# A kernel's own account of VectorE's time: shorter prices, a catch-up after forced steps, and one more chunk for the seven-product pair

## The chip, the cores and the metric

The kernel runs on one core of one Trainium2 chip. The metric is the device time of one execution in microseconds (us), the median of several runs. TensorE (PE in the profile) multiplies matrices, VectorE (DVE) and ScalarE (ACT) work element by element, GpSimd (POOL) does little here, and SyncE (SP) issues nearly all DMAs.

## What is computed

The reference is one step of a two-layer streaming encoder over 1024 prompt rows and 32 sample rows, with 1024 channels. Cut to what matters, each layer does this:

```
mod = silu(c) @ w_ada[i] + b_ada[i]            # 6 vectors a layer: shifts, scales, gates
h   = rmsnorm(x) * (1 + sc1) + sh1
mix = layer 0: spatial gating, (u * (W_s v + b)) @ w_out
      layer 1: trailing means over 2, 4, 8, 16 rows minus the row, then a map for each group
x   = x + gt1 * rmsnorm(mix)
h   = rmsnorm(x) * (1 + sc2) + sh2
x   = x + gt2 * rmsnorm(square(relu(h @ w_up)) @ w_down)     # 1024 -> 4096 -> 1024
```

Everything is float32. The last 15 inputs of the pooling mixer and the normalised v of the sample rows are outputs too.

## The kernel before

**Tiles.** Channels lie on the partitions. The 1056 rows are three tiles of 384, 384 and 288 columns (t = 0, 1, 2; the last has the sample rows). Each float32 operand is split into a high part, rounded by ScalarE, and a low part, subtracted on VectorE, and a product takes three matmuls (high by high, high by low, low by high: `products`, lines 1047 to 1049).

**Order of the large products.** First v of the gating mixer (`v_mm`, `v_end`), then u, the gate and the output map (`sgu_item`, `gate`: matmuls at line 1401, their input `vl` loaded at line 1355), then both feed-forward nets. A feed-forward net is cut into eight chunks of 512 hidden channels, c = 0 to 7. The list `passes` (lines 374 to 383) says in which order chunks meet tiles: an entry is (layer, first chunk, tiles, number of chunks). Some entries take tiles 0 and 1 together (`PAIR`). There `pair_item` (from line 1551) writes h @ w_up as a 2 by 2 block product with seven block products in place of eight (lines 1586 to 1588), on sums of blocks: `combos` builds the sums of h, `quads` (line 494) those of the weights. The products by w_down are plain. In layer 0 the pair takes chunks 3 to 7, in layer 1 chunks 2 to 7. What remains of chunks 0 to 2 is done for single tiles, and tile 2 takes all its chunks alone, after the pair.

**Weights.** `stream` holds all loads in order: weights, and the pieces of w_ada ("wide" pieces and their folds, `do_ada`, with a small matmul at line 649), which `some_ada` strews between the chunks. Raw pieces have three buffers; the split parts sixteen slots.

**The planner.** The order in which instructions are written decides who waits, since each engine works in order (a scheduling layer may still move some of them). The kernel plans with an account, `time`, of two sums: `time["pe"]` grows by `tick` at each product, `time["dve"]` by a price for each VectorE instruction, set in `on_dve` (lines 74 to 87) as a fixed part plus elements over a rate:

```
    tt = on_dve(nc.vector.tensor_tensor, 0.16, 930.0)
    stt = on_dve(nc.vector.scalar_tensor_tensor, 0.16, 840.0)
```

Work that must only be done by some later time (normalising, residual additions, pooling, output) stands in generators, `fillers`. After each product `weave` takes one or two steps of the weight stream, unless VectorE is ahead in the account (`stream_waits`), and then filler steps for as long as the account of VectorE stands behind TensorE's:

```
        while time["dve"] < time["pe"] and fillers:
            if not pull():
                break
```

A step may set a gate: the next one then opens only when `time["pe"]` has passed. Before a tile's first chunk of a layer, `run_ffn` calls `finish`, which pulls all that is left of that tile's filler at once:

```
    def finish(tag):
        while any(f[0] == tag for f in fillers):
            pull(True)
```

The fillers that matter here: `ffn0_t` (from the mixer to the input of layer 0's net for tile t), `ffn1_t` (`to_pool`: from layer 0's net through the pooling mixer to the input of layer 1's net), `combos`, and `state`, `sgu_state` (line 1276), which for four quarters loads `vst` and `gvb`, multiplies them on VectorE and stores the product. Its tiles, and `vl`, come from the three buffers of the tag x3.

Of the kernel before, what the change touches and what calls it, by code (L numbers as in the profile page):

```python
# [35 lines left out]
def tile_stream_encoder_step(  # L36
# [25 lines left out]
    nc = tc.nc  # L62
# [5 lines left out]
    time = {"pe": 0.0, "dve": 0.0}  # L68
# [5 lines left out]
    def on_dve(op, fixed, rate):  # L74
        def run(out, *args, **kw):
            n = 1
            for k in out.shape[1:]:
                n *= k
            time["dve"] += fixed + n / rate
            return op(out, *args, **kw)  # L80

        return run

    tt = on_dve(nc.vector.tensor_tensor, 0.16, 930.0)
    stt = on_dve(nc.vector.scalar_tensor_tensor, 0.16, 840.0)
    ts = on_dve(nc.vector.tensor_scalar, 0.1, 930.0)
    turn32 = on_dve(nc.vector.transpose, 0.1, 930.0)

    def pool(name, **kw):
        return ctx.enter_context(tc.tile_pool(name=name, bufs=1, reuse_waits="tile", **kw))  # L90
# [52 lines left out]
    def ps_ms(name):  # L143
        return psum.tile([P, 512], F32, tag="pm", bufs=3, name=name)
# [207 lines left out]
    def w_chunk(n):  # L352
        l, c, tiles, m = passes[n]
        for j in range(4 * m):
            f = 4 * c + j
            add_w(
                ("up", n, j),
                ffn_w_up[l][:, f * P : (f + 1) * P].rearrange("(k p) f -> p k f", p=P),
                (8, P),
                ("one", "two")[j % 2] if tiles == PAIR else "w",  # L360
            )
        w = 256 // m
        for q in range(4 * m):
            add_w(
                ("dn", n, q),
                ffn_w_down[l][c * 512 : (c + m) * 512, q * w : (q + 1) * w].rearrange(
                    "(j p) d -> p j d", p=P
                ),
                (4 * m, w),
            )  # L370

    every = list(range(NT))
    PAIR = every[:2]
    passes = [(0, 0, [0], 2), (0, 2, [0], 1)]
    passes += [(0, c, [1], 1) for c in range(3)]
    passes += [(0, c, PAIR, 1) for c in range(3, 8)]
    passes += [(0, c, [NT - 1], 2) for c in (0, 2, 4, 6)]
    passes += [(1, 0, [0], 2)]
    passes += [(1, c, [1], 1) for c in range(2)]
# [6 lines left out]
    def some_ada(n):  # L386
        for _ in range(min(n, len(rest))):
            add, l, j = rest.pop(0)
            add(l, j)
# [29 lines left out]
    for n, (l, c, tiles, m) in enumerate(passes):  # L419
        w_chunk(n)  # L420
        if tiles == PAIR:
            some_ada((5, 2)[l])
        elif l == 0 and tiles != [NT - 1] and c > 0:
            some_ada(c + 1 if tiles == [1] else 2)
    some_ada(99)
# [120 lines left out]
    def ada_finish(l, sl, view):  # L546

        nk = 2 * view.shape[1]
        m = mod[:, l, 2 * sl : 2 * sl + nk, :].rearrange("p (s h) v -> p s h v", h=2)
        b = bT[:, l * 48 + 2 * sl : l * 48 + 2 * sl + nk].rearrange("p (s h) -> p s h", h=2)  # L550
        tt(out=m, in0=view, in1=b.unsqueeze(3).broadcast_to([P, nk // 2, 2, NV]), op=ALU.add)
        which, k0 = sl // 4, 2 * (sl % 4)
        slot = {1: (0, 0), 2: (1, 1), 4: (2, 2), 5: (3, 3)}.get(which)
        if slot is not None:
            cf, gi = slot
            for v in range(NV):
                stt(
                    out=coef[:, l, cf, v, k0 : k0 + nk],
                    in0=mod[:, l, 2 * sl : 2 * sl + nk, v],
                    scalar=1.0 if cf in (0, 2) else 0.0,  # L560
                    in1=g_of(l, gi)[:, k0 : k0 + nk],
                    op0=ALU.add,
                    op1=ALU.mult,
                )
# [40 lines left out]
    def do_ada(l, sl, q, r, w):  # L605
        nq = w // 128
        if q == 0:
            aas = [
                work.tile([P, 512], F32, tag="aa", bufs=2, name=f"aa{l}_{sl}_{w}_{i}")
                for i in range(nq // 2)  # L610
            ]
            ada_acc[0] = [aas[v * nq // 4][:, v * w % 512 :][:, :w] for v in range(NV)]
        aa = ada_acc[0]
        for c in range(8 // nq):
            for v in range(NV):
                x = r[:, c * w : (c + 1) * w]
                k = csil[:, 8 // nq * q + c, v : v + 1]
                if q == 0 and c == 0:
                    with tc.issue_after(last_lo[("v", 1, 3)].ins):
                        ts(aa[v], x, k, None, op0=ALU.mult)  # L620
                else:
                    stt(out=aa[v], in0=x, scalar=k, in1=aa[v], op0=ALU.mult, op1=ALU.add)
        if q < nq - 1:
            return


        ns = nq // 2
        i = sl * ns % 4
        if i == 0 and state["folds"]:
            run_deferred(True)  # L630
        for v in range(NV):
            turned = r[:, v * w : (v + 1) * w]
            turn32(turned, aa[v])
            time["dve"] += 0.16 + w / 840.0
            nc.vector.tensor_reduce(
                out=part[:, i : i + ns, v],
                in_=turned.rearrange("p (s b m) -> p s b m", s=ns, m=32),
                op=ALU.add,
                axis=AX.X,
            )  # L640
        if i + ns < 4:
            return
        state["folds"] = 1

        def fold():
            state["folds"] = 0
            pa = ps_ms(f"ada{l}_{sl}")
            for c in range(4):
                mm(
                    pa[32 * c : 32 * c + 32, :16],  # L650
                    quad,
                    part.rearrange("p s v (h c) -> p c (s v h)", c=4)[:, c],
                    start=True,
                    stop=True,
                    tile_position=(0, 32 * c),
                    skip_group_check=True,
                )
            y = pa[:, :16].rearrange("p (s v h) -> p s h v", s=4, v=NV)
            ada_finish(l, (sl + 1) * ns - 4, y)

        defer(fold, fold_lag[0])
# [3 lines left out]
    def defer(step, us=None):  # L665

        at = 0.0 if us is None else max(time["pe"], time["dve"]) + us
        deferred.append((at, step))

    def run_deferred(force=False):  # L670
        n = len(deferred)
        while n > 0 and (force or deferred[0][0] <= time["pe"]):
            deferred.pop(0)[1]()
            n -= 1
# [39 lines left out]
    def stream_step():  # L714
# [17 lines left out]
        if kind == "w":  # L732
            do_w(key, r)
        elif kind == "wide":
            do_ada(*key, r, 512)
        elif kind == "ada":
            if k < first_ada:
                do_ada_pe(*key, r)
            else:
                do_ada(*key, r, 256)  # L740
        else:
            do_x(key, r)
# [35 lines left out]
    def pull(force=False):  # L778

        def open_(f):
            return force or gates.get(f[0], 0.0) <= time["pe"]

        if sticky:
            f = sticky[-1]
            if not open_(f):
                return False
            sticky.pop()
        else:  # L790
            f = next((f for f in list(fillers)[:2] if open_(f)), None)
            if f is None:
                return False
        try:
            step = next(f[1])
        except StopIteration:
            fillers.remove(f)
            return True
        if step is True:
            sticky.append(f)  # L800
        elif step is not False:
            gates[f[0]] = max(time["pe"], time["dve"]) + step
        return True
# [12 lines left out]
    def finish(tag):  # L816
        while any(f[0] == tag for f in fillers):
            pull(True)


    def spread(t, ss, tag, out, dg):
# [729 lines left out]
    def pair_item(p, after, ends):  # L1551
# [48 lines left out]
        def up(jp):  # L1600
# [10 lines left out]
            if jp == 0:  # L1611
                flush()
                finish("combos")
# [56 lines left out]
        if passes[p + 1][2] != PAIR:  # L1670
            finish(f"ffn{l}_{NT - 1}")
            fillers.append(late_norm.pop())
# [277 lines left out]
    def run_ffn(l, after):  # L1950
        for p, (pl, c, tiles, m) in enumerate(passes):
            if pl != l:
                continue
            ends = [t for t in tiles if not any(q[0] == l and t in q[2] for q in passes[p + 1 :])]
            if tiles == PAIR:
                pair_item(p, after, ends)
                continue
            for t in tiles:
                if c == 0:
                    if any(f[0] == f"ffn{l}_{t}" for f in fillers):  # L1960
                        flush()
                    finish(f"ffn{l}_{t}")
                ffn_item(p, t, after if t in ends else None)
# [158 lines left out]
```

## Time and profile before

| what | value |
|---|---|
| median of 3 runs | 2157.3 us (2157.04 to 2158.1) |
| the profiled execution, its own time | 2154.9 us |
| its span, first to last instruction | 2153.1 us |
| TensorE busy | 2102.8 us |
| weight loads of TensorE (PEld) | 2032.5 us |
| VectorE busy | 1560.3 us |
| ScalarE busy | 1041.6 us |
| mean granted TensorE clock | 0.99 |
| read from and written to memory | 274.76 MB and 30.66 MB |

The span is the time between the first and the last instruction of the profiled execution; 1.8 us of its own time lie around it, and that time is 2.4 us under the median. Busy time of TensorE overlaps between matmuls that follow each other, so that a matmul's mean duration is longer than the distance between two starts. The clock column gives the share of the full TensorE clock that was granted.

### The profile page before, as it was taken

To read this page: it belongs to the slowest core of one execution; us is meant where nothing else is said; L and a number is where in the kernel's file an instruction comes from. 1 tells how busy PE (TensorE), PEld (TensorE's weight loads), DVE (VectorE), ACT (ScalarE), POOL (GpSimd) and SP (SyncE) were. 2 spreads that over 40 slices of the span, in tenths; PEclk is the share of its full clock that TensorE was granted. 3 is DMA by queue.
4 is the path that set the end of the run, shared out by engine and by line. 5 is a ranking of instruction groups with operands and counts; after the bars stand their busy time and mean duration, and the time that the engine had idled before them with its cause. 6 is when DMAs were issued, how large, how long until landed. Compare 5 with 4: busy or idle time off the path is not lost.

```text
span 2153.1 us, 32925 instructions
## 1 busy us (share of the span) xinstructions
PE 2102.8 (98%) x12858; PEld 2032.5 (94%) x12858; DVE 1560.3 (72%) x2756; ACT 1041.6 (48%) x1833; POOL 22.4 (1%) x44
## 2 busy tenths in 40 slices
PE   8999999999999999999998999896999999999998
PEld 6878999999999999999998999896999999999998
DVE  6778837567778857878777887849677768579554
ACT  5634431233456545334455756555445454365555
POOL 0000000000000000000000000000000000001100
PEclk9999999999999999999999999998999999999999
DMA  8576524353445443334335775643342323238873
GB/s 290 169 256 210 179 81 136 97 163 109 122 129 167 138 147 121 105 98 128 108 122 146 214 221 145 191 131 104 89 142 90 91 86 101 69 113 224 203 188 92
DMA packets 424050, 307.59 MB, mean 143 GB/s; under 512 B 47023, under 2 KB 387287, under 8 KB 423893
## 3 DMA queue, kind: packets, MB, share of 16 engines
q1 hardware_dynamic: 422964, 304.19, 47.2%
q8 instruction: 101, 1.65, 0.3%
q0 software_dynamic: 896, 1.28, 0.2%
q14 instruction: 57, 0.46, 0.1%
q10 hardware_dynamic: 32, 0.01, 0.0%
HBM read 274.76 MB, written 30.66 MB: 142 GB/s over the span
## 4 chain that ended last, share of the span: by engine, by line
PE 90%; DVE 5%; DMA 2%; ACT 2%; issue 1%; DVEq 0%; ACTq 0%
PE pg L1048 10%; PE pg L1047 10%; PE pg L1049 10%; PE pf L1047 5%; PE pf L1048 5%; PE pf L1049 5%; PE pu L1047 3%; PE pu L1049 3%; PE pu L1048 3%; PE po L1047 3%; PE po L1049 3%; PE po L1048 3%; PE pfa L1586 3%; PE pfa L1588 3%; PE pfa L1587 3%; PE pv L1073 2%
## 5 line engine op out<-in xcount | busy, mean ns | idle before, releaser
L1047 PE MATMUL pg<-fh,wh_dn 128*128 128x384 f32 (+1 forms) x968 | 314.7, 326 | 0.9 <-DVE acc L80 0.9
L1048 PE MATMUL pg<-fl,wh_dn 128*128 128x384 f32 (+1 forms) x968 | 312.9, 323 | 0.0
L1049 PE MATMUL pg<-fh,wl_dn 128*128 128x384 f32 (+1 forms) x968 | 311.9, 323 | 0.0
L80 DVE TENSOR_TENSOR wl_dn<-raw,wh_dn 128x1024 fp32r<-128x1024 f32 x148 | 181.1, 1224 | 140.3 <-ACT wh_dn L533 92.9
L1047 PE MATMUL pf<-hh,wh_up 128*128 128x288 f32 (+1 forms) x832 | 262.4, 316 | 10.0 <-ACT hh L1007 8.4
L1048 PE MATMUL pf<-hl,wh_up 128*128 128x288 f32 (+1 forms) x832 | 260.8, 314 | 0.0
L1049 PE MATMUL pf<-hh,wl_up 128*128 128x288 f32 (+1 forms) x832 | 260.1, 313 | 0.0
L533 ACT ACTIVATE wh_dn<-raw 128x1024 fp32r<-128x1024 f32 x148 | 156.7, 1059 | 152.2 <-PE pf L1048 65.1
L80 DVE SCALAR_TENSOR_TENSOR aa<-raw,csil,aa 128x512 f32<-128x512 f32 (+1 forms) x364 | 206.2, 620 | 4.5 <-DMA raw<-in_w_ada_dram 4.4
L80 DVE TENSOR_TENSOR acc<-acc,pg 128x384 f32<-128x384 f32 (+1 forms) x256 | 134.7, 531 | 85.7 <-PE pg L1049 84.4
L1047 PEld LDWEIGHTS pg<-fh,wh_dn 128*128 128x128 f32 x968 | 181.5, 188 | 2.6 <-DVE acc L80 1.3
L1048 PEld LDWEIGHTS pg<-fl,wh_dn 128*128 128x128 f32 x968 | 181.7, 188 | 1.0 <-DVE fl L80 0.2
L1049 PEld LDWEIGHTS pg<-fh,wl_dn 128*128 128x128 f32 x968 | 181.6, 188 | 0.0
L533 ACT ACTIVATE wh_up<-raw 128x1024 fp32r<-128x1024 f32 x104 | 110.2, 1059 | 127.1 <-PE pg L1048 76.2
L80 DVE TENSOR_TENSOR wl_up<-raw,wh_up 128x1024 fp32r<-128x1024 f32 x104 | 126.8, 1220 | 61.1 <-ACT wh_up L533 60.6
L1047 PEld LDWEIGHTS pf<-hh,wh_up 128*128 128x128 f32 x832 | 158.5, 191 | 12.6 <-ACT hh L1007 9.2
L1048 PEld LDWEIGHTS pf<-hl,wh_up 128*128 128x128 f32 x832 | 158.4, 190 | 1.1 <-DVE hl L80 0.9
L1049 PEld LDWEIGHTS pf<-hh,wl_up 128*128 128x128 f32 x832 | 158.8, 191 | 0.1
L1047 PE MATMUL pg<-fx,wh_dn 128*128 128x288 f32 (+1 forms) x392 | 121.8, 311 | 0.0
L1048 PE MATMUL pg<-fx,wh_dn 128*128 128x288 f32 (+1 forms) x392 | 121.7, 311 | 0.0
L1049 PE MATMUL pg<-fx,wl_dn 128*128 128x288 f32 (+1 forms) x392 | 121.4, 310 | 0.0
L1047 PE MATMUL po<-ush,wh_o 128*128 128x384 f32 (+1 forms) x288 | 92.6, 322 | 0.0
(408 smaller groups left out, 5112.3 us busy)
## 6 DMA issues: line engine op xcount, KB each, us to landing
raw<-in_ffn_w_up_dram SPq DMA_DIRECT2D x148, 512.0 KB, 4.0
raw<-in_ffn_w_down_dram SPq DMA_DIRECT2D x148, 512.0 KB, 4.1
raw<-in_w_ada_dram SPq DMA_DIRECT2D x90, 512.0 KB, 4.2
raw<-in_sgu_w_in_dram SPq DMA_DIRECT2D x40, 512.0 KB, 4.0
xd<-acc SPq DMA_DIRECT2D x8, 1536.0 KB, 7.4
raw<-in_sgu_w_out_dram SPq DMA_DIRECT2D x24, 512.0 KB, 3.6
xo_r<-xd SPq DMA_DIRECT2D x32, 384.0 KB, 4.1
vd<-vt SPq DMA_DIRECT2D x32, 256.0 KB, 4.4
```

Source lines behind the costliest of these rows:

```text
L80: return op(out, *args, **kw)
L533: act(out=wh, in_=r, func=AF.Copy)
L1047: mm(ps[:, :n], wh, rh, start=i == 0, stop=False)
L1048: mm(ps[:, :n], wh, rl, start=False, stop=False)
L1049: mm(ps[:, :n], wl, rh, start=False, stop=i == last)
L1073: mm(ps[:m, :], a_h, wh[:, o : o + 512], start=k == 0, stop=False)
L1586: mm(ps[:, :n], wh[:, o], rh, start=first and k == 0, stop=False, skip_group_check=True)
L1587: mm(ps[:, :n], wh[:, o], rl, start=False, stop=False, skip_group_check=True)
L1588: mm(ps[:, :n], wl[:, o], rh, start=False, stop=k == HK - 1, skip_group_check=True)
```

## The change

Three things change.

The prices of VectorE's instructions in the account become smaller. For 512 elements a `stt` goes from 0.77 to 0.67 us, for 1024 elements a `tt` from 1.26 to 1.15 us.

`finish` brings the account of TensorE up to 3 us behind VectorE's when it has pulled its steps.

In layer 0 the pair takes chunk 2 as well: the single entries of chunk 2 for tiles 0 and 1 go. `some_ada` puts six wide pieces behind each pair chunk of layer 0 but the last in place of five, and one behind the last.

```diff
-    tt = on_dve(nc.vector.tensor_tensor, 0.16, 930.0)
-    stt = on_dve(nc.vector.scalar_tensor_tensor, 0.16, 840.0)
-    ts = on_dve(nc.vector.tensor_scalar, 0.1, 930.0)
-    turn32 = on_dve(nc.vector.transpose, 0.1, 930.0)
+    tt = on_dve(nc.vector.tensor_tensor, 0.07, 950.0)
+    stt = on_dve(nc.vector.scalar_tensor_tensor, 0.13, 950.0)
+    ts = on_dve(nc.vector.tensor_scalar, 0.13, 1900.0)
+    turn32 = on_dve(nc.vector.transpose, 0.06, 880.0)
...
-    passes = [(0, 0, [0], 2), (0, 2, [0], 1)]
-    passes += [(0, c, [1], 1) for c in range(3)]
-    passes += [(0, c, PAIR, 1) for c in range(3, 8)]
+    passes = [(0, 0, [0], 2)]
+    passes += [(0, c, [1], 1) for c in range(2)]
+    passes += [(0, c, PAIR, 1) for c in range(2, 8)]
...
         if tiles == PAIR:
-            some_ada((5, 2)[l])
+            some_ada(2 if l else 6 if c < 7 else 1)
...
-            time["dve"] += 0.16 + w / 840.0
+            time["dve"] += 0.06 + w / 950.0
...
     def finish(tag):
         while any(f[0] == tag for f in fillers):
             pull(True)
+        time["pe"] = max(time["pe"], time["dve"] - 3.0)
```

## The prediction

> **What bounds the kernel now.** The page first. The second row tells that TensorE is busy nearly always, so time can only come from fewer matmuls or from the stretches in which it stands still or runs slowly; the third shows where the clock was not fully granted.
>
> ```profile
> span 2153.1 us, 32925 instructions
> PE 2102.8 (98%) x12858; PEld 2032.5 (94%) x12858; DVE 1560.3 (72%) x2756; ACT 1041.6 (48%) x1833; POOL 22.4 (1%) x44
> ...
> PEclk9999999999999999999999999998999999999999
> ```
>
> Then TensorE's own waits: what it waited for, in all, times, longest.
>
> ```profile
> PE pn_r_1x L920 <- ACT sc_r_1x L873: 12.5, 1, 12.5
> PE pf L1047 <- ACT hh L1007: 8.4, 2, 4.3
> PE ada L649 <- DVE part L635: 5.8, 2, 5.5
> ...
> PE pn_r_0x L920 <- ACT sc_r_0x L873: 3.1, 1, 3.1
> ```
>
> These four rows hold 29.8 us. All belong to the way from one net to the next: a norm's sum (pn), the first input of layer 1's net (hh), a fold of w_ada. Last, the busy times by stretch, around those waits (the first row is plain pair work, for its pace):
>
> ```profile
> core 0: us, PE busy (x) PEld busy (x) DVE busy (x) ACT busy (x) POOL busy (x), PEclk, DMA share, GB/s
> ...
> 894.00:923.00 29.00, 29.00 (x170) 28.95 (x169) 17.71 (x26) 17.94 (x34) 0.00 (x0) 1.00 0.38 119
> 1145.00:1157.00 12.00, 6.50 (x36) 6.25 (x35) 9.45 (x18) 4.16 (x6) 0.00 (x0) 0.72 0.45 126
> 1157.00:1257.00 100.00, 99.76 (x749) 99.18 (x748) 83.95 (x116) 66.11 (x109) 0.00 (x0) 1.00 0.71 206
> 1257.00:1314.00 57.00, 57.00 (x409) 54.88 (x409) 37.27 (x50) 32.98 (x53) 0.00 (x0) 1.00 0.71 211
> 1314.00:1371.00 57.00, 56.81 (x404) 54.24 (x403) 56.79 (x85) 41.07 (x70) 0.00 (x0) 1.00 0.63 189
> 1371.00:1385.00 14.00, 6.79 (x22) 5.56 (x22) 11.76 (x21) 6.98 (x13) 0.00 (x0) 0.65 0.66 194
> 1385.00:1416.00 31.00, 31.00 (x179) 31.00 (x179) 14.63 (x18) 18.48 (x30) 0.00 (x0) 0.99 0.38 107
> 1416.00:1460.00 44.00, 44.00 (x227) 39.61 (x226) 22.08 (x39) 22.70 (x38) 0.00 (x0) 1.00 0.41 129
> 1460.00:1484.00 24.00, 7.13 (x20) 5.72 (x19) 23.12 (x38) 10.50 (x17) 0.00 (x0) 0.58 0.36 115
> ```
>
> The reader is to see three holes and one oddity. In 1145:1157, 1371:1385 and 1460:1484 TensorE starts 36, 22 and 20 matmuls; at the pace of the rows beside them (100.00/749 = 0.134 us for tile 2, 31.00/179 = 0.173 us for 384 columns) these need 4.8, 3.8 and 3.5 us. The holes cost 7.2 + 10.2 + 20.5 = **37.9 us**, half clock after each included (clock 0.72, 0.65, 0.58). The oddity: between the second and third hole, in 1385:1460, VectorE is busy for 36.7 of 75 us, and in the third it is full (23.12 of 24). The work that TensorE waits for could have been done earlier.
>
> The account explains that. Counted while the program is built, `finish` has to pull 6 steps of `ffn0_2` (first hole), 23 of `ffn1_0` (second) and 21 of `ffn1_1` (third), and 6 of layer 1's `combos`. After the 23 the account has VectorE 23 us ahead of TensorE, though TensorE really waited; so no filler is pulled for that long.
>
> **The change part by part.**
>
> *The prices.* Two views price VectorE: mean duration by shape, and starts of equal instructions back to back (timeline row, then two rows of the chain).
>
> ```profile
> L80 DVE TENSOR_TENSOR wl_dn<-raw,wh_dn 128x1024 fp32r<-128x1024 f32 x148 | 181.1, 1224 | 140.3 <-ACT wh_dn L533 92.9 <-PE pfb L1587 42.2 <-issue 5.0
> L80 DVE SCALAR_TENSOR_TENSOR aa<-raw,csil,aa 128x512 f32<-128x512 f32 x196 | 137.5, 744 | 1.1 <-DMA raw<-in_w_ada_dram 1.0
> ```
> ```profile
> 860.30 2.07 DVE L80 SCALAR_TENSOR_TENSOR aa<-raw,csil,aa 128x512 f32<-128x512 f32 x3
> ```
> ```profile
> 1314.26 4.16 DVE acc L80 x8
> ...
> 1320.79 1.14 DVE wl_up L80
> ```
>
> A 512-element `stt` starts the next after (2.07 - 0.744)/2 = 0.66 us (old price 0.77, new 0.67); a 1024-element `tt` takes 1.14 us of the chain (1.26, 1.15); a 384-element `stt` 4.16/8 = 0.52 us (0.62, 0.53). The old prices are 11 to 19% over the interval, the new ones 1 to 3%. So the old account thought VectorE full where 1157:1257 has it at 84%; with the new one fillers come earlier. In the changed program no step is left for any of those `finish` calls. All of tile 0's and tile 1's preparation for layer 1, the pooling matmuls included, stands inside tile 2's passes of layer 0; only tile 1's last norm product stands at the border, just before layer 1's first product. The first hole's fold stands inside the pair's chunk 6.
>
> What this asks of VectorE: every VectorE instruction of both programs from the pair's last product to the end of layer 0's net, at these intervals, gives 184 us before (the four stretches 1145 to 1371 show 187.5 busy) and 204 us after, beside 224 us of TensorE at its pace (10 more than before, the moved pooling matmuls). VectorE then stands at 91%. Bounds for what TensorE loses to that: in 1314:1371 VectorE was busy for 56.79 of 57 us and TensorE lost 0.2; at the other end VectorE never gets over the 84% of 1157:1257, which would take 204/0.84 = 243 us, a loss of 19. I take 2.5 us, near the row with VectorE full, because it is the only one in which VectorE really had no pause. Gain of the three holes: **-37.9**, loss inside the passes **+2.5** (0 to 19).
>
> *The catch-up in `finish`.* With nothing forced it changes nothing by itself; if steps were forced after all, it would let VectorE work on in the stretch after them. Cost 0; its cover is the absence of forced steps.
>
> *Chunk 2 in the pair.* For two tiles, up takes 7 block products of 12 matmuls, twice: 168 in place of 192. 24 matmuls at 29.00/170 = 0.171 us: **-4.1 us**, all on TensorE's path. Eight weight loads of 512 KB and eight splits on ScalarE and VectorE go, the pair's sums come, and all in all VectorE has 12 more `tt`. The five pair passes of layer 0 before:
>
> ```profile
> 816.00:1145.00 329.00, 327.41 (x1901) 325.83 (x1902) 255.92 (x423) 140.38 (x262) 0.00 (x0) 1.00 0.35 108
> ```
>
> VectorE is at 78% there (255.92 of 329), so 12 `tt` of at most 0.6 us find room. Cost nothing.
>
> *Wide pieces.* Six in place of five behind a pair chunk put four 512-element `stt`, about 2.7 us, into 66 us with 14 us of pause: hidden, and the first hole's fold is done by then. Without that pause, 2.7 us a chunk.
>
> *The table loads.* The changed program has two more on ScalarE:
>
> ```profile
> L924 ACT ACT_TABLE_LOAD x4 | 5.1, 1283 | 0.1
> ```
>
> 2.6 us on an engine that is busy for 48% of the time; nothing on the path.
>
> *What gets worse: the filler `state`.* The new account calls for all four of its steps before tile 0's second gate input, `vl`, is asked for. In SP's queue `vl` now stands behind four `vst`, four `gvb` and three stores, and its buffer is that of the third `vst`, whose store must land first. Rows of before: the two `vl` loads at 222.66, gates at 230.21 and 240.54, one store and the `gvb` that waited for it, then the loads' time to landing (min/median/max).
>
> ```profile
> 222.66 0.99 SPq L1355 DMA_DIRECT2D vl<-vd  x2
> ...
> 236.15 0.34 SPq L1292 DMA_DIRECT2D out_dram<-vst  x1
> ...
> 238.39 0.32 SPq L1281 DMA_DIRECT2D gvb<-in_sgu_g_v_dram  x1
> ```
> ```profile
> 230.37 1.34 PE psp L1401 x12
> 240.54 1.34 PE psp L1401 x12
> ```
> ```profile
> L1355 SPq DMA_DIRECT2D vl<-vd x24: 359/367/772, 222.7 to 571.3; - x24
> ...
> DMA to landing us min/median/max: 2.4/4.1/7.0
> ```
> ```profile
> L80 DVE SCALAR_TENSOR_TENSOR vst<-vst,rv,gvb x4: 729/734/740, 235.4 to 256.7; 32x512 f32<-32x512 f32 x4
> ...
> DMA to landing us min/median/max: 1.9/2.5/3.6
> ```
>
> From the first gate's end (231.7) VectorE does the gate's work and the first quarter by 234.3; each further quarter needs a store (238.39 - 236.15 = 2.2), a `gvb` (2.5) or VectorE's queue, about 5 us: the third is done at 244.6, its store lands at 247.0, `vl` lands 2.4, 4.1 or 7.0 later: 249.4, 251.3 or 254.2. TensorE has been given two more u products ahead of this gate, 48 matmuls or 8.3 us after 240.5: it comes at 248.8. Wait 0.6 to 5.4, at the median **+2.5 us**.
>
> *Sum* against the profiled execution's own time, 2154.9: -37.9 - 4.1 + 2.5 + 2.5 = -37.0, so 2117.9. The median of the runs is 2.4 us above that execution: 2120.3, rounded **2120 us**, 1.7% faster.
>
> **A rule on the clock.** The rows say: after 5.5 us without a matmul, the clock stays low for a while.
>
> ```profile
> 1145.89 0.29 PE L1048 MATMUL pf<-hl,wh_up 128*128 128x288 f32 x1
> 1151.69 0.31 PE L649 MATMUL ada<-part,quad 128*32 128x16 f32 x8 [5.50 <-DVE part L635]
> ...
> 1153.30 0.44 PE L1047 MATMUL pf<-hh,wh_up 128*128 128x288 f32 x1
> 1153.54 0.44 PE L1048 MATMUL pf<-hl,wh_up 128*128 128x288 f32 x1
> ```
>
> Afterwards 288 columns start every 0.24 us in place of 0.134, until about 1156.6: (1156.6 - 1153.1) x 0.44 = 1.6 us lost. The Trainium skill, TensorE: Matmul & The Clock Gate, "HAM oscillation", says that idle gaps of TensorE over some 3.4 us bring the half clock; the trace agrees, as the longest waits in the holes, 5.5, 4.3 and 12.5 us, are longer. It speaks against this change at one place: if the new wait at the gate passes that length, a stretch that ran at full clock now halves. At the median wait of 2.5 us the sum stays as it is by that rule; at 5.4 us it becomes the first rival's.
>
> **The rivals.**
> - *The gate's wait is long and halves the clock* (0.08): 5.4 us in place of 2.5, and some 2 us after it, as in the first hole: 2120 + 5 = 2125. For it: `vl` has landed as late as 7.0 us after its issue. Against: the median.
> - *VectorE keeps its 16% of pauses* in tile 2's passes (0.15): +19 in place of +2.5: 2137. For it: VectorE waits in order behind ScalarE's halves and TensorE's results (140.3 us of idle time ahead of `wl_dn` alone), and the new prices count no wait. Against: 1314:1371.
> - *VectorE becomes the bound; slower than before* (0.05): if in those passes it reaches only its share of the whole span, 72%, it needs 204/0.72 = 283 us beside 224: +59 in place of +2.5, 2177. It decides where 204/share exceeds 224 by the 39.5 us that the holes and the matmuls bring less the gate's wait, at a share under 0.77. Against it: 1157:1257 had 84% with TensorE stopped for 0.24 us.
> - *It doesn't do what it says* (0.04): the forced steps go, but the same instructions are late by as much, as norm sums stand ahead of the products that could run; only the 24 matmuls remain: 2153.
> - *Nothing new waits* (0.06): neither gate nor passes, 2120 - 5, and the waits where passes meet shrink as well: about 2113.
>
> **How the numbers follow.** The forecast, 2120 (own bounds 2113 to 2128), gets 0.62. Range 2106 to 2137: down to 2106 if other small waits go too, up to the second rival's 2137; it leaves out the two bad cases and the far half of the second, about 0.17. Faster by over 0.2% (about what a measurement here can tell from no change): 0.62 + 0.08 + 0.15 + 0.06 = 0.91; the fourth rival, -4.1 us, lies at the bound: 0.04 same; 0.05 slower.
>
> **What would show it.** TensorE's waits lose the rows of 12.5, 8.4 and 5.5 us, and the clock is 1.00 over those stretches; VectorE is at 90% or more in tile 2's passes of layer 0 and TensorE's busy share there stays over 98%. The gate in the stretch that begins at 240 shows a wait of 0.6 to 5.4 us on `vl`, none before. The pair's chunk 2 has 168 up matmuls. I am wrong if TensorE's waits name VectorE's sums (`acc`, `fl`, `hl`) inside tile 2's passes for more than 5 us in all, or if layer 1's first products still wait on a norm.

## The result and the profile after

| | before | after |
|---|---|---|
| median | 2157.7 us (4 runs) | 2125.8 us (2124.5 to 2127.7, 4 runs) |
| ratio to before | | 0.9853, interval 0.9835 to 0.987 |
| the profiled execution, its own time | 2154.9 us | 2127.7 us |
| its span | 2153.1 us | 2125.9 us |

The change makes the kernel 1.5% faster. The forecast was 2120, with a range of 2106 to 2137. The page of the kernel after, the rows that answer to those of before:

```profile
span 2125.9 us, 32854 instructions
PE 2096.6 (99%) x12834; PEld 2024.1 (95%) x12834; DVE 1558.5 (73%) x2768; ACT 1036.7 (49%) x1841; POOL 22.3 (1%) x44
...
PEclk9999999999999999999999999999999999999999
```

TensorE starts 24 matmuls fewer, and the dip of the clock row is gone. The waits of TensorE after (in all, times, longest):

```profile
PE xT L686 <- DMA x_rows<-in_x_prompt_dram: 4.9, 1, 4.9
PE pfb L1587 <- ACT wh_up_S L508: 3.4, 1, 3.4
PE pfa L1587 <- ACT a L1593: 3.0, 4, 0.9
PE pv L1120 <- ACT hh L1008: 1.8, 2, 1.1
PE psp L1402 <- DMA vl<-vd: 1.2, 1, 1.2
```

The rows of 12.5, 8.4, 5.8 and 3.1 us are gone: no norm, no first input of layer 1 and no fold is waited for, but for 0.2 us each on a norm's sum and a fold. There are three new rows, a weight (`wh_up_S`, 3.4), ScalarE's copy of `pfa` (`a`, 3.0 in four waits) and the gate's `vl` (1.2). The same stretches as before, after the change:

```profile
core 0: us, PE busy (x) PEld busy (x) DVE busy (x) ACT busy (x) POOL busy (x), PEclk, DMA share, GB/s
1145.00:1157.00 12.00, 12.00 (x85) 12.00 (x85) 8.07 (x12) 8.07 (x16) 0.00 (x0) 1.00 0.44 127
1157.00:1257.00 100.00, 99.17 (x698) 94.25 (x697) 91.48 (x136) 72.17 (x124) 0.00 (x0) 1.00 0.68 207
1257.00:1314.00 57.00, 57.00 (x417) 55.69 (x417) 52.25 (x71) 34.94 (x55) 0.00 (x0) 1.00 0.75 228
1314.00:1371.00 57.00, 56.79 (x388) 52.83 (x387) 48.14 (x76) 42.13 (x75) 0.00 (x0) 1.00 0.57 176
1371.00:1385.00 14.00, 14.00 (x95) 14.00 (x94) 13.07 (x20) 8.72 (x15) 0.00 (x0) 1.00 0.80 223
1385.00:1416.00 31.00, 31.00 (x181) 31.00 (x181) 25.75 (x49) 21.36 (x39) 0.00 (x0) 1.00 0.45 127
...
1460.00:1484.00 24.00, 24.00 (x138) 23.52 (x137) 22.49 (x33) 16.75 (x32) 0.00 (x0) 1.00 0.57 177
```

The three holes are full of matmuls at full clock, with VectorE at 91% in 1157:1257, 92% in 1257:1314 and 84% in 1314:1371. But the span fell by 27.2 us, not by 37.0. (The medians fell by 31.9 us: the traced execution before was 2.8 us under its median, the one after 1.9 us over it.) Where TensorE loses time is told by a sum over its stretches: each runs from the start of one named matmul to the start of another in the trace, and what it lasts beyond its matmuls at their pace (0.173 us for 384 columns, 0.133 for 288, 0.227 for 512; the pooling's matmuls `pp`, at 0.32 for 384 and 0.24 for 288, and smaller ones at theirs) is lost.

| lost by TensorE, us | before | after | difference |
|---|---|---|---|
| start to first u | 8.8 | 10.8 | +1.9 |
| gating mixer | 1.1 | 3.3 | +2.2 |
| layer 0, single tiles | 2.5 | 2.0 | -0.4 |
| layer 0, pair | 4.9 | 7.3 | +2.5 |
| layer 0, tile 2 (first hole) | 8.9 | 2.3 | -6.6 |
| layer 1, up to the pair (second and third hole) | 33.1 | 1.2 | -31.8 |
| layer 1, pair, chunks 2 and 3 | 0.9 | 11.8 | **+10.9** |
| layer 1, the rest | 7.0 | 5.4 | -1.6 |
| 24 matmuls | | | -4.2 |

But for rounding the differences add up to -27.2. What is missing against the forecast, 9.8 us, is about the size of one new hole, in a stretch that the prediction did not look at. The chain of waits after shows how it comes about (start, duration, what):

```profile
1550.42 2.73 DVE aa L80 x4
1553.15 0.60 DVE acc L80 x2
1553.75 0.17 DVE win2s L80
1553.92 0.46 DVE acc L80
1554.38 0.16 DVE win2s L80
1554.54 1.14 DVE wl_up_A L80
...
1556.61 0.60 DVE raw L80
1557.21 0.15 DVE win2s L80
1557.36 0.61 DVE raw L80
1557.98 0.02 issue
1558.00 0.64 ACT wh_up_S L508
1558.64 0.04 issue
1558.68 0.69 PE pfb L1587
```

From 1550.42 VectorE works without a pause: on a wide piece (`aa`), on tile 2's pooling (`win2s`, and part of `acc`; the rest of `acc` adds up chunk 2's products), on the low part of a weight (`wl_up_A`) and on the sums of chunk 3's weights (`raw`). TensorE waits for these sums, split by ScalarE, until 1558.68. Two stretches of the trace after, the second nearly all at half clock (it runs from 1557.40 to 1564.23):

```profile
1545.00:1557.15 12.15, 9.00 (x49) 8.02 (x47) 11.37 (x26) 3.73 (x7) 0.00 (x0) 1.00 0.46 133
1557.15:1563.98 6.83, 5.30 (x16) 5.11 (x17) 4.12 (x13) 1.26 (x2) 0.00 (x0) 0.52 0.13 38
```

Why TensorE waits although other work is left is told by the order of its instructions. `down` writes all 192 `pg` matmuls of chunk 2 ahead of chunk 3's first. The scheduling layer left 60 of them in front, and put 16 matmuls of chunk 3 before the other 132. The next of these 132 read nothing of chunk 3, but they stand behind `pfb`, and TensorE takes its matmuls in this order. No run tells how early they could have run.

### The profile page after: what moved, and what is told of

Same layout as the page of the kernel before. It is cut to its first block, busy times and chain, and to the rows that moved or that the text cites. A ratio compares the mean times of both kernels' runs of the same rounds, so it can differ in the third digit from the quotient of the medians.

```text
span 2125.9 us, 32854 instructions
## 1 busy us (share of the span) xinstructions
PE 2096.6 (99%) x12834; PEld 2024.1 (95%) x12834; DVE 1558.5 (73%) x2768; ACT 1036.7 (49%) x1841; POOL 22.3 (1%) x44
## 4 chain that ended last, share of the span: by engine, by line
PE 58%; DVE 5%; ACT 3%; DMA 2%; issue 1%; DVEq 0%; ACTq 0%; SPq 0%
PE pg L1049 10%; PE pg L1048 10%; PE pg L1050 10%; PE pf L1048 4%; PE pf L1050 4%; PE pf L1049 4%; PE pfa L1587 2%; PE pfa L1588 2%; PE pfa L1589 2%; PE pfb L1587 1%; PE pfb L1588 1%; PE pfb L1589 1%; PE pp L1941 1%; DMA raw<-in_ffn_w_up_dram 1%; DVE aa L80 1%; DVE acc L80 1%
## 5 line engine op out<-in xcount | busy, mean ns | idle before, releaser
L1048 PE MATMUL pg<-fh,wh_dn 128*128 128x384 f32 (+1 forms) x944 | 306.4, 325 | 1.2 <-DVE acc L80 0.9
L1048 PE MATMUL pf<-hh,wh_up 128*128 128x288 f32 (+1 forms) x768 | 238.1, 310 | 0.0
L1049 PE MATMUL pf<-hl,wh_up 128*128 128x288 f32 (+1 forms) x768 | 236.6, 308 | 0.0
L1050 PE MATMUL pf<-hh,wl_up 128*128 128x288 f32 (+1 forms) x768 | 236.4, 308 | 0.0
L533 ACT ACTIVATE wh_up<-raw 128x1024 fp32r<-128x1024 f32 x96 | 101.7, 1059 | 99.3 <-PE pg L1049 60.5
L80 DVE TENSOR_TENSOR wl_up<-raw,wh_up 128x1024 fp32r<-128x1024 f32 x96 | 117.1, 1219 | 42.7 <-ACT wh_up L533 42.4
L1048 PEld LDWEIGHTS pf<-hh,wh_up 128*128 128x128 f32 x768 | 144.0, 188 | 0.9 <-ACT wh_up L533 0.5
L1050 PEld LDWEIGHTS pf<-hh,wl_up 128*128 128x128 f32 x768 | 144.4, 188 | 0.4 <-DVE wl_up L80 0.4
L1049 PEld LDWEIGHTS pf<-hl,wh_up 128*128 128x128 f32 x768 | 144.2, 188 | 0.4
L491 ACT ACTIVATE wh_up_A<-raw 128x1024 fp32r<-128x1024 f32 (+1 forms) x48 | 39.3, 837 | 135.3 <-DMA raw<-in_ffn_w_up_dram 95.2
```

Of the source, the lines that this page charges most:

```text
L491: act(out=wh, in_=r, func=AF.Copy)
L533: act(out=wh, in_=r, func=AF.Copy)
L1048: mm(ps[:, :n], wh, rh, start=i == 0, stop=False)
L1049: mm(ps[:, :n], wh, rl, start=False, stop=False)
L1050: mm(ps[:, :n], wl, rh, start=False, stop=i == last)
```

## The experiments

Three groups of four kernels ran on three chips, each beside the kernel before (medians 2154.8, 2155.2 and 2155.5 us). The ratios are of mean times. Forced steps are counted while a program is built.

| kernel | median us | ratio to before | interval |
|---|---|---|---|
| e1: prices alone | 2128.2 | 0.9870 | 0.9852 to 0.9887 |
| e2: chunk 2 alone | 2147.3 | 0.9960 | 0.9944 to 0.9976 |
| e3: catch-up alone | 2126.4 | 0.9861 | 0.9845 to 0.9876 |
| e4: wide pieces alone | 2129.3 | 0.9876 | 0.9861 to 0.9892 |
| e5: after, tile 2's filler held | 2121.1 | 0.9841 | 0.9827 to 0.9854 |
| e6: after, wide pieces off the border | 2122.2 | 0.9847 | 0.9834 to 0.9861 |
| e7: e5, and a gate in `state` | 2119.1 | 0.9832 | 0.9818 to 0.9845 |
| e8: after, old prices | 2110.0 | 0.9793 | 0.9780 to 0.9807 |
| e9: after, again | 2127.1 | 0.9864 | 0.9851 to 0.9878 |
| e10: chunk 2 and wide pieces | 2113.3 | 0.9804 | 0.9790 to 0.9817 |
| e11: after, prices half way | 2114.4 | 0.9812 | 0.9798 to 0.9825 |
| e12: after, old price of `tt` | 2114.0 | 0.9806 | 0.9792 to 0.9819 |

The theory was that forced steps make the three holes, and that the prices make the forced steps. The rivals were that the mere amount of VectorE's work, or another part of the change, decides.

**e1, the prices alone.** The five lines with prices and nothing else.

```diff
-    tt = on_dve(nc.vector.tensor_tensor, 0.16, 930.0)
+    tt = on_dve(nc.vector.tensor_tensor, 0.07, 950.0)
...
-            time["dve"] += 0.16 + w / 840.0
+            time["dve"] += 0.06 + w / 950.0
```

> Only the five prices are changed; chunk 2, the wide pieces and the catch-up stay as before. While it is built, finish has to pull 5 steps ahead of tile 2's first chunk of layer 0, and none later. Theory (the holes come from steps that are pulled too late, because the account thinks VectorE full): the second and third hole go, 31 us, the first stays or shrinks; against it new waits like those of the changed kernel, some 10 us in layer 1's pair: 2125 to 2138 us. Rival (VectorE simply has too much to do around tile 2's passes, so that only less work there helps): the waits move to other places, 2150 us or more.

2128.2 us. Five steps of `ffn0_2` are still forced, none in layer 1, and TensorE loses 1.0 us in place of 33.1 on the way to layer 1's pair, though VectorE runs the same number of instructions (2756). So the amount of work is not the cause. Tile 2's passes of layer 0, with the five forced steps ahead of them, still lose 5.2 us of 8.9. The pair's chunks 2 and 3 of layer 1 lose 9.5 us in place of 0.9, so a new hole comes with the prices. It is one chunk later: six matmuls of chunk 4 stand ahead of the last 84 of chunk 3, and TensorE waits 2.9 us for their weight `wl_up_A`.

**e2, chunk 2 alone.** The pair takes chunk 2, with five wide pieces behind every chunk as before.

```diff
-    passes = [(0, 0, [0], 2), (0, 2, [0], 1)]
-    passes += [(0, c, [1], 1) for c in range(3)]
-    passes += [(0, c, PAIR, 1) for c in range(3, 8)]
+    passes = [(0, 0, [0], 2)]
+    passes += [(0, c, [1], 1) for c in range(2)]
+    passes += [(0, c, PAIR, 1) for c in range(2, 8)]
```

> Only chunk 2 goes into layer 0's pair; prices, wide pieces (five behind a pair chunk) and finish as before. Forced steps are as before: 6, 23, 21 and 6. Theory: the three holes stay, 24 matmuls go, 4 us: 2151 to 2156 us. Rival (less VectorE work by eight splits is what fills the holes): 2140 us or less.

2147.3 us, 4 us under the expected range, with a span 7.0 us shorter: 4.2 are the matmuls, the rest is spread over small differences. The forced steps are those of before (6, 23, 21), and so are the waits of TensorE in this kernel:

```profile
PE pn_r_1x L920 <- ACT sc_r_1x L873: 12.5, 1, 12.5
PE pf L1047 <- ACT hh L1007: 8.1, 2, 4.3
PE ada L649 <- DVE part L635: 5.0, 2, 4.8
```

**e3, the catch-up alone.** One line in `finish`, at the old prices.

```diff
+        time["pe"] = max(time["pe"], time["dve"] - 3.0)
```

> Only the line in finish is added. Forced steps: 8 ahead of tile 2, 8 of ffn1_0, none of ffn1_1 and of the sums. Theory: the third hole (20 us) goes, since VectorE's account no longer stands 23 us ahead after the second; the first stays, the second is half: 2130 to 2140 us. Rival (VectorE's amount of work sets it): 2150 us or more.

2126.4 us, better than expected. In `ffn1_0` 8 steps are forced in place of 23, in `ffn1_1` and `combos` none. With the account brought level after the first forced steps, VectorE works on, and the later calls find nothing to force. Lost on the way to layer 1's pair: 1.6 us. Tile 2's passes of layer 0, with 8 steps forced ahead of them, still lose 6.9 us of 8.9.

**e4, the wide pieces alone.**

```diff
-            some_ada((5, 2)[l])
+            some_ada(2 if l else 6 if c < 7 else 1)
```

> Only the wide pieces: six behind each pair chunk of layer 0 and one behind the last, so that four of them leave the beginning of tile 2's passes. Forced steps: 4, 12, 12, none of the sums. Theory: the holes shrink about as the forced steps, to some 60%: 2140 to 2148 us. If wide pieces cost and bring nothing, as I had them: 2157 us.

2129.3 us, 11 us under the expected range. The forced steps fall to 4, 12 and 12, and tile 2's passes of layer 0 lose 2.2 us in place of 8.9. With five pair chunks the number of pieces is the same, 25: behind chunks 3 to 6 stands one more each, behind chunk 7 four fewer. So four pieces, 16 `stt` of 0.66 us or 10.6 us of VectorE, leave the border of the pair and tile 2's passes, where VectorE is short of time, for the pair's chunks, where it has pauses. 11.7 us are still lost on the way to layer 1's pair; the waits of layer 1's first products are the largest left there (5.4 us in all, the longest 4.3):

```profile
PE pf L1047 <- ACT hh L1007: 5.4, 2, 4.3
```

**e5, tile 2's filler held until chunk 3.** To the new hole: is it made by the filler `ffn1_2` or by the wide pieces at that border?

```diff
+        if l == 1 and c == 3:
+            combined.append(1)
...
-                while len(combined) < 2:
+                while len(combined) < 3:
```

> The changed kernel, but tile 2's filler of layer 1 (ffn1_2) may not begin before the pair's chunk 3 of layer 1. Theory (in the pair's chunk 2 of layer 1 VectorE has this filler to do beside the chunk's sums, so the weights' sums for chunk 3 come late, and the hole of 3.6 us with the half clock behind it at the border of chunks 2 and 3 follows): the wait on wh_up_S of 3.4 us goes, the chunk loses under 1 us in place of 9, the filler makes chunk 3 lose 2 to 3 us; time 2115 to 2119, against 2125.8. Rival (the two wide pieces that stand at this border hold the raw buffers, or VectorE, whatever the filler does): the wait stays over 2 us, time 2123 to 2127.

2121.1 us, 2 us over the expected range. The wait on `wh_up_S` is gone and chunk 2 loses 0.1 us in place of 9.0. But the filler now stands in chunk 4, which loses 5.6; the expectation had 2 to 3 in chunk 3. The three chunks of this kernel:

```profile
1512.70:1573.00 60.30, 60.30 (x350) 60.30 (x349) 44.30 (x72) 28.46 (x50) 0.00 (x0) 1.00 0.42 131
1573.00:1637.50 64.50, 64.22 (x374) 63.63 (x373) 49.45 (x92) 31.69 (x64) 0.00 (x0) 1.00 0.28 82
1637.50:1714.40 76.90, 72.66 (x396) 68.34 (x395) 61.46 (x124) 37.55 (x72) 0.00 (x0) 1.00 0.38 112
```

`combined` counts the sets of `combos` that are made; the filler begins when there are enough. The filler has to do with the hole, but moving it as a lump moves half of the loss along.

**e6, no wide pieces at that border.**

```diff
-            some_ada(2 if l else 6 if c < 7 else 1)
+            some_ada((0, 2, 4)[(c > 2) + (c == 4)] if l else 6 if c < 7 else 1)
```

> The changed kernel, but no wide pieces stand behind the pair's chunk 2 of layer 1; its two come behind chunk 4. Theory (the filler makes the hole): the wait on wh_up_S shrinks by no more than the pieces' own time on VectorE, some 3 us, so by the end of the half clock at most 5 us are won; time 2120 to 2126. Rival (the wide pieces make it): the hole goes as a whole, time 2115 to 2118.

2122.2 us. The wait on `wh_up_S` shrinks from 3.4 to 0.5, so the pieces do delay the sums. Chunks 2 and 3 still lose 7.3 us of 11.8, for here too the layer puts 24 matmuls of chunk 3 among chunk 2's, and TensorE then waits for the pooling weights `wg`. Neither filler nor pieces make the hole alone: both are queued on VectorE at the same place.

**e7, e5 with a gate in `state`.** One line more, in `sgu_state`:

```diff
-            yield False
+            yield 12.0
```

> The changed kernel with two edits: ffn1_2 held until the pair's chunk 3 of layer 1, and a gate of 12 us behind each step of the filler state, so that the second load of vl stands ahead of most of that filler's loads in SP's queue. Theory: 9 us by the first edit, 1 to 2 by the second; the wait of psp on vl goes; time 2114 to 2117. Rival (the wait on vl only moves to another load of this stage, and the hole stays): 2123 to 2126.

2119.1 us, 2 us over the expected range. The wait on `vl` (1.1 us in e5) is gone, and the mixer loses 1.3 us in place of 3.3: the wait was made by the loads and stores of `state` ahead of `vl`. The times alone do not show it, since the intervals of e5 and e7 overlap.

**e8, the old prices with the rest of the change.** All prices as before; the other parts as in the changed kernel.

```diff
-    tt = on_dve(nc.vector.tensor_tensor, 0.07, 950.0)
+    tt = on_dve(nc.vector.tensor_tensor, 0.16, 930.0)
...
-            time["dve"] += 0.06 + w / 950.0
+            time["dve"] += 0.16 + w / 840.0
```

> The change without its prices: the old prices, the catch-up, chunk 2 in the pair of layer 0 with its six wide pieces. 1 step of ffn0_2 and 6 of ffn1_0 are still forced. Theory (the old prices with the catch-up spread tile 2's filler of layer 1 over chunks 2 and 3, so no hole at that border, and the gate of layer 0 keeps its place; the kernel with the catch-up alone took 2126.4, its trace 2120.9): 4 us of matmuls less than that, 2116 to 2123, faster than the whole change. Rival (the prices are what brings the gain, and chunk 2 brings the new waits): over 2126.

2110.0 us, the fastest of all, below what was expected, and 17 us by the medians under e9, which differs from it in the prices alone (each beside the kernel before on its own chip; the intervals lie apart). Chunks 2 and 3 lose nothing (-0.3 by the paces), the mixer 1.2. The two chunks after (first two rows) and in e8 (last two):

```profile
1514.70:1597.20 82.50, 77.02 (x408) 72.97 (x407) 61.64 (x122) 37.24 (x72) 0.00 (x0) 0.96 0.32 96
1597.20:1658.70 61.50, 60.15 (x342) 58.74 (x341) 48.56 (x91) 27.57 (x51) 0.00 (x0) 1.00 0.37 105
```
```profile
1508.90:1570.30 61.40, 61.40 (x360) 61.12 (x359) 50.81 (x93) 30.49 (x63) 0.00 (x0) 1.00 0.31 91
1570.30:1641.00 70.70, 70.70 (x396) 68.73 (x395) 59.81 (x121) 36.23 (x70) 0.00 (x0) 1.00 0.38 112
```

VectorE does the same there (110.2 and 110.6 us) in 12 us less. What differs is when the sums are ready and when they are asked for. In e8 the split of the sums, and the first matmul with it:

```profile
1549.30 0.63 ACT L508 ACTIVATE wh_up_S<-raw 128x512 fp32r<-128x512 f32 x1 [2.77 <-DVE raw L80]
```
```profile
1572.82 0.33 PE L1587 MATMUL pfb<-hh,wh_up_S 128*128 128x384 f32 x1
```

The split begins 23.5 us ahead of the matmul. Counted from the first of chunk 2's products by w_down (the unbroken run from 1537.45 in e8, from 1543.19 after), it comes 11.9 us later in e8 and 14.8 us later in the changed kernel. But TensorE asks for it 35.4 us later in e8, and after 12.1 us in the changed kernel. So the sums are some 3 us later there, and they are asked for 23 us earlier: most of the difference is the order of the matmuls. In e8 all 192 matmuls of chunk 2 come before chunk 3's, and the pooling products come among chunk 3's first ones.

**e9, the changed kernel again.**

> The changed kernel itself, once more, on the chip and beside the runs of the three kernels that follow. Theory (the 10 us by which its trace lies over the sum come from the program): 0.984 to 0.987 of the kernel before, the wait on wh_up_S of over 2 us again at the border of chunks 2 and 3 of layer 1's pair, the wait on vl again, but less than 10.8 us lost before the first u product, as the first loads come at chance. Rival (that hole was an accident of one execution): no wait on wh_up_S over 1 us, the time at 0.980 to 0.982.

2127.1 us; its trace has the same two waits (3.4 on `wh_up_S`, 1.3 on `vl`) and loses 11.8 us in chunks 2 and 3. The hole belongs to the program.

**e10, the third part alone.** Chunk 2 in the pair and the wide pieces: the diffs of e2 and e4 together.

> The third part of the change alone: chunk 2 in the pair of layer 0 and six wide pieces behind a chunk, at the old prices and without the catch-up. Forced: 1 step of ffn0_2, 6 of ffn1_0, 5 of ffn1_1 (before: 6, 23, 21). The kernel with this part and the catch-up took 2110.0. Theory (few forced steps leave little for a catch-up to mend; the holes shrink with the number of forced steps): 2110 to 2120, that is 0.979 to 0.984. Rival (the holes need the catch-up or the prices; this part is worth the matmuls and the wide pieces' 26 us less what remains of forced steps): 2122 to 2130, waits of layer 1's first products on a norm or on hh over 4 us.

2113.3 us, without the new prices and without the catch-up. Forced: 1, 6 and 5 steps. On the way to layer 1's pair 2.2 us are lost. e2 and e10 differ in the wide pieces only, by 34 us: with the pair longer by a chunk, as without it, the four pieces behind chunk 7 decide whether `finish` has to force.

**e11, prices half way.**

```diff
-    tt = on_dve(nc.vector.tensor_tensor, 0.07, 950.0)
-    stt = on_dve(nc.vector.scalar_tensor_tensor, 0.13, 950.0)
+    tt = on_dve(nc.vector.tensor_tensor, 0.11, 940.0)
+    stt = on_dve(nc.vector.scalar_tensor_tensor, 0.15, 890.0)
...
```

> The changed kernel, with prices about half way between the old and the new: 0.11 + n/940 for tt, 0.15 + n/890 for stt, so 5 to 10% over the intervals. No step is forced in layer 0 or layer 1's first chunks. Theory (the new prices hold nothing back for the time in which VectorE waits, so the filler is pulled faster than VectorE can do it, and weights' sums behind it come late; some reserve spreads it): the loss in the pair's chunks 2 and 3 of layer 1 falls from 11.8 us to 2 to 5, time 2110 to 2118. Rival (only the place of tile 2's filler in the chunk counts, and here most of it still stands in chunk 2): loss 8 us or more there, 2120 to 2127.

2114.4 us; chunks 2 and 3 lose 3.6. Only 6 matmuls of chunk 3 stand among chunk 2's.

**e12, the old price of `tt` alone.**

```diff
-    tt = on_dve(nc.vector.tensor_tensor, 0.07, 950.0)
+    tt = on_dve(nc.vector.tensor_tensor, 0.16, 930.0)
```

> The changed kernel, but the price of tt alone is the old one (0.16 + n/930). No step is forced before the output. 18 of the pooling products come only behind the pair's chunk 2 of layer 1, in the changed kernel within it. Theory (tt is what the weights' sums and the splits are counted by; with its reserve the filler keeps clear of them): loss in chunks 2 and 3 of 2 us or less, time 2108 to 2116. Rival (the weights' sums come late through the wide pieces, priced as stt): the wait on wh_up_S stays, 2120 to 2127.

2114.0 us; chunks 2 and 3 lose 1.0, and the order of chunk 2's 192 matmuls is whole, as in e8. The old price of `tt` alone brings 13 of the 17 us: the weights' sums and splits and much of the pooling are counted by it. The old price of `stt` alone was not tried.

## Why the prediction was right, and where it was wrong

- **The three holes: right.** -38.4 us in the two rows of the table that hold them, against -37.9 + 2.5. The cause is shown: e1, e3 and e4 change different things, all lower the number of forced steps, and all close the second and third hole or most of them (33.1 us lost becomes 1.0, 1.6 and 11.7); e2 leaves the steps and the holes. The first hole's row falls less in e1 and e3 (to 5.2 and 6.9 us of 8.9), where 5 and 8 steps are still forced.
- **VectorE in tile 2's passes: right, with the term a little large.** 91% was expected; 1157:1371 shows 192 of 214 us, 90%, with 84% in its last part. Tile 2's passes lose 2.3 us in all. Of the 8.9 us before, 7.2 were the hole by the prediction, so 1.7 were lost beside it already: 0.6 us came, the term was 2.5. No wait on VectorE's sums over 5 us stands there.
- **The gate: right.** The wait on `vl` is 1.2 us, within the 0.6 to 5.4 and under the 2.5 of the term; the mixer as a whole loses 2.2 us more. The row after, with `vl` waited for:

```profile
252.01 1.24 PE L1402 MATMUL psp<-wr,vl 128*128 128x128 f32 x9 [1.23 <-DMA vl<-vd]
```

The clock stayed at 1.00 there.
- **The catch-up at nothing: as far as the runs show.** The changed kernel has no forced step at the calls in question, so the line has nothing to mend there; the changed kernel without it was not run. Alone it is worth 1.4% (e3), and beside the third part, at the old prices, too little to tell (e8 against e10, with overlapping intervals).
- **Chunk 2 at -4.1: right for the matmuls** (24 fewer, 4.2 us at their pace). Its cover was a little dearer: the pair of layer 0 loses 2.5 us more, most of it in waits on ScalarE's copy of `pfa` (the row of 3.0 us above; three of its four times stand there). This isn't chunk 2's price: e2, with chunk 2 and five wide pieces, has no such wait there, nor has e4, with six pieces and without chunk 2. In e10, which has both, they come to 2.5 us in four waits, at the old prices. So they come with the six pieces in the longer pair.
- **"Wide pieces ... hidden": the step that failed first.** It counted the four `stt` that come to each chunk (which beside chunk 2 were not quite hidden, by the point above), and not that four pieces leave chunk 7. Alone that brings 26 us (e4), and with chunk 2 it brings nearly all there is (e10). The forecast came out right because the gain was put down to the prices, which close the holes too (e1), and the holes can be closed only once. That the time fell within the forecast's own bounds is in part luck, since the loss in the next point was missing from the sum.
- **The prices: a term is missing.** "With the new one fillers come earlier" was counted as a gain only. The prediction did see that the new prices "count no wait" and put the loss of that into tile 2's passes. It fell in layer 1's pair, +10.9 us in chunks 2 and 3. With the other parts in place the prices take back 17 us by the medians (e8 against e9). Of the 17.4 us between the two traces, 1.8 are the start of the kernel: the first u product starts at 221.73 and 223.54. Over all traces this start lies between 221.7 and 223.9, early and late with either prices, so it is not theirs.

Of the rivals, the long wait at the gate, the pauses in tile 2's passes, VectorE as the bound, "doesn't do what it says" and "nothing new waits" did not come. The second came near in its mechanism (the new prices count no wait) and was wrong in its place.

What stays open: why the layer puts matmuls of chunk 3 among chunk 2's in some programs and not in others, and so by which way the prices make the new hole (the layer's own estimate of times was not looked at); and what six wide pieces in place of five are worth in the changed kernel itself, which was not tried.

## What to carry to other kernels

An exact price is not always the better one for a planner: here prices 1 to 3% over an instruction's interval were slower than prices 5 to 19% over it, once the holes were closed (e9 against e8 and e11). A price near the interval leaves nothing for the waits between instructions; that work without hurry then crowds out what the bottleneck needs next is the likely reason, and only a part of it was measured. When work moves, count the place that it leaves as well as the place where it arrives. When several parts of a change could close the same hole, try each alone before giving one of them the gain.

## What was not expected of the hardware

Away from the kernel's end, the half clock came in stretches of 3.41, 6.83, 10.24 and 20.48 us. With the wait of 3.4 us in the changed kernel came 6.83 us at half clock, from 1557.40 on, that is from 1.3 us before the wait ended. A shorter wait can do it: in e6 a wait of 2.21 us, and 3.41 us at half clock from 0.2 us before its end on.

```profile
1565.31 3.75 PE L1941 MATMUL pp<-acc,wg 128*128 128x288 f32 x8 [2.21 <-DMA wg<-in_pool_w_grp_dram]
```
```profile
1565.07:1568.48 3.41, 3.17 (x7) 2.35 (x8) 0.00 (x0) 0.00 (x0) 0.00 (x0) 0.50 0.00 0
```

The kernel before shows it as well. In its second hole the half clock began at 1375.31, behind a wait of 3.13 us; the wait of 4.08 us on `hh` came only after that.

```profile
1374.50 0.44 PE L920 MATMUL pn_r_0x<-sc_r_0x,ones 128*128 128x384 f32 x1 [3.13 <-ACT sc_r_0x L873]
```
```profile
1371.90:1375.31 3.41, 0.81 (x4) 0.63 (x4) 2.09 (x5) 1.72 (x4) 0.00 (x0) 1.00 1.11 325
1375.31:1385.55 10.24, 6.16 (x18) 5.34 (x19) 9.31 (x17) 5.32 (x11) 0.00 (x0) 0.50 0.45 143
```

And in e3 no wait was over 0.8 us. TensorE was busy for 1.92 of 3.41 us, and 3.41 us at half clock followed:

```profile
1146.46:1149.87 3.41, 1.92 (x12) 1.36 (x11) 3.41 (x11) 2.47 (x4) 0.00 (x0) 1.00 0.76 215
1149.87:1153.28 3.41, 3.41 (x16) 3.41 (x15) 3.41 (x14) 1.44 (x2) 0.00 (x0) 0.50 0.48 141
```

The 1.23 us at the gate left the clock at 1.00, and so did single waits of 1.7 us in e1 and e7. So the length of one wait alone does not decide; how little TensorE works within a stretch may, which no run tested. The Trainium skill, TensorE: Matmul & The Clock Gate, "HAM oscillation", puts the limit at gaps over some 3.4 us; the wait of 3.4 us agrees with it, but here a wait of 2.21 us was enough. The prediction's "the trace agrees" holds for the first and third hole, and not for the second.
